# One decode of the expert picks for eight heads in 16 bits, in place of two for four heads in 32 bits

## The chip, the cores and the metric

One core of one Trainium2 chip runs the whole program as one launch. The metric is the device time of that launch in microseconds; the median of several runs counts. Times inside a profile are counted from the first instruction (the span's start).

## What is computed

Two decoder blocks over 256 tokens of width 1024. The first ends in a feed-forward layer of 16384 experts, of which every token uses 16 for each of 8 heads. The part that matters here, cut from the reference:

```python
def peer_ffn(xn, wq, subkeys, u_tab, v_tab):
    q = (xt @ wq).reshape(T, PEER_HEADS, 2, PEER_HALF)
    s = jnp.einsum('thpd,hpnd->thpn', q, subkeys).astype(jnp.float32)
    top_s, top_i = lax.top_k(s, PEER_TOPK)                     # 16 of 128 row keys, 16 of 128 column keys
    cand_s = (top_s[:, :, 0, :, None] + top_s[:, :, 1, None, :]).reshape(...)
    cand_i = (top_i[:, :, 0, :, None] * PEER_NKEYS + top_i[:, :, 1, None, :]).reshape(...)
    best_s, best_j = lax.top_k(cand_s, PEER_TOPK)              # 16 of the 256 pairs
    idx = jnp.take_along_axis(cand_i, best_j, axis=-1)
    gates = jax.nn.softmax(best_s, axis=-1)
    def retrieve(args):
        uc, vc = u_tab[ic], v_tab[ic]
        hdn = jax.nn.gelu(jnp.einsum('cd,chkd->chk', xc, uc), approximate=False) * gc
        return jnp.einsum('chk,chkd->cd', hdn, vc)
```

The kernel does not gather. It multiplies all experts with all tokens ("ups", table `peer_u`), weighs each hidden unit with a dense gate that is zero for experts not picked, and multiplies with the second table ("downs", `peer_v`).

## The kernel before, in words

Matrix products of 32-bit weights are made from a high and a low part: ScalarE writes `whi` from the loaded slice `raw`, VectorE or GpSimd the rest `wlo` = `raw` - `whi` (`split_next`, line 452). Each slice has 128x1024 numbers; four raw slices and four split pairs fit. Weights are loaded and split in the fixed order of the list `order`, ahead of their use.

The program is written out by one planner, `Flow` (line 107), which keeps a model clock per engine. Matrix work comes from a list of jobs. Beside them run chains (Python generators); after each piece of matrix work the planner steps every chain whose time has come by the model clock of TensorE. `yield 0` waits until the model says that the chain's last results are there, `yield SOON` lets it go on 1.2 us before that. So the order of instructions on each engine is fixed when the program is built; on the chip, engines wait for one another's data.

The feed-forward layer goes so. The query products of the 8 heads come first. For every head, `top_keys` (line 1597) scores the keys; `best16` (line 1579) finds the 16 best with VectorE's max and index instructions; GpSimd adds the 56 candidate pairs that can win into `cd`, and `best16` picks 16 of them into `bs` (values) and `bj` (positions, 0 to 63). After head 7 the two chains `decode(0)` and `decode(1)` (line 1629) follow one another, each for four heads. A decode

- subtracts the largest value (`g_`), and takes from the position, by shifts, casts, comparisons and small products on [128, 2, 16, 4] tiles, which of the 16 row keys and of the 16 column keys it names (`row`, `cl`): 25 VectorE instructions, lines 1637 to 1675;
- looks the key numbers up, in four passes (two token halves, row and column): compare `row` or `cl` with the constant table `io16` (filled by GpSimd in `top_keys` for head 1, line 1600), multiply with the 16 key numbers `il`, add the 16 products in halves, write into `GI` (lines 1678 to 1692). These run on 16-bit tiles of [128, 16, 64];
- makes Exp of `g_` on ScalarE, and on VectorE the softmax sum, the gate and its rest behind 16 bits (lines 1694 to 1703).

After the second decode TensorE transposes the eight parts of `GI`, and ScalarE writes them into `GT` (lines 1706 to 1713). `ex["gates"]` counts these steps; at 3 `swap_pools` (line 1899) gives the decode's memory to the gate tiles, and `dense_gates` (line 1877) starts. It builds the dense gates in four blocks of 32 key rows. `gate_steps` (line 1827) makes, for 8 tokens at a time, the one-hot tiles `oq`, `oe` and `op` on VectorE, and TensorE multiplies them: 16 small products for block 0, a "burst"; ScalarE copies them out into `gd`. A block has 32 such steps.

The order of the experts is given by hand (lines 893 to 897): ups 0 to 21 (`LEAD` 16 plus `AHEAD` 6), then downs 0 to 5, then up and down in turn. Down 0 waits until block 0 is built (`ex["built"]`, line 1804); `weigh` (line 1739) multiplies the hidden units with the gates on VectorE and makes the high part `ah` on ScalarE and the low part `al` on VectorE. Block 1 may start after six downs (line 1884) and is needed for down 16. From the first decode to the last gate block all `wlo` are VectorE's (`pool_free`, line 464).

Of the kernel before, what the change touches and what calls it, by code (L numbers as in the profile page):

```python
# [10 lines left out]
F32 = mybir.dt.float32  # L11
F32R = mybir.dt.float32r
F16 = mybir.dt.float16
# [299 lines left out]
def tile_blocks(ctx: ExitStack, tc: tile.TileContext, a, out):  # L313
# [32 lines left out]
    def bank(tag="sm"):  # L346
        return psum["tiles"].tile([128, 512], F32, name=tag, tag=tag, bufs=psum[tag])
# [13 lines left out]
    def cst(name):  # L361
        k, s, e = TABS[name]
        return tabs[k][:, s:e]
# [1175 lines left out]
    def open_c():  # L1539
        nonlocal sk, io16, v16, i16, bs, bj, GI  # L1540
        pa.__exit__(None, None, None)
        banks(4, 4)
        Bt.open(tc.tile_pool(name="pbt", bufs=1, side="right", reuse_waits="tile"))
        sk = Bt.tile([128, 16, 128], F32, name="sk")
        nc.scalar.dma_start(sk, a["sk"])
        io16 = Bt.tile([128, 16, 64], F16, name="io16")
        v16 = Bt.tile([128, 2, 16, 16], F32, name="v16")
        i16 = Bt.tile([128, 2, 16, 16], U32, name="i16")
        bs = Bt.tile([128, 2, 8, 16], F32, name="bs")
        bj = Bt.tile([128, 2, 8, 16], U32, name="bj")  # L1550
        GI = [Bt.tile([128, 4, 2, 64], F32, name="GI%d" % tt) for tt in range(2)]
        yield


# [42 lines left out]
    def top_keys(h, q):  # L1597
        yield lambda: ex["top"] == h and ex["best"] >= h - 1 and ex["sums16"] >= h - 2
        if h == 1:
            G.tensor_copy(io16, cst("iota16")[:, :, None].to_broadcast([128, 16, 64]))  # L1600
        b = bank()
        for tt in range(2):
            for p_ in range(2):
                o = (tt * 2 + p_) * 128
                mm(b[:, o:o + 128], q[:, p_, tt * 128:(tt + 1) * 128], sk[:, 2 * h + p_, :])
        s_ = Bt.tile([128, 4, 128], F32, name="s_", tag="s_", bufs=2)
        S.activation(s_, b4(b), AF.Copy)
        ex["top"] += 1
        yield 0
        yield lambda: ex["best"] == h  # L1610
        yield from best16([(v16[:, tt, 2 * h + p_, :], i16[:, tt, 2 * h + p_, :], s_[:, tt * 2 + p_, :])
                for tt in range(2) for p_ in range(2)], 128)
        ex["best"] += 1


        cd = Bt.tile([128, 2, 64], F32, name="cd", tag="cd", bufs=2)
        for i0, n, w, o in ((0, 1, 16, 0), (1, 3, 8, 16), (4, 4, 4, 40), (8, 8, 1, 56)):
            G.tensor_tensor(cd[:, :, o:o + n * w].rearrange("p t (i j) -> p t i j", i=n),
                            v16[:, :, 2 * h, i0:i0 + n, None].to_broadcast([128, 2, n, w]),
                            v16[:, :, 2 * h + 1, None, 0:w].to_broadcast([128, 2, n, w]), op=OP.add)  # L1620
        yield 0
        yield lambda: ex["sums16"] == h
        yield from best16([(bs[:, tt, h, :], bj[:, tt, h, :], cd[:, tt, :]) for tt in range(2)], 64)
        ex["sums16"] += 1
        if h == 7:
            for g in range(2):
                flow.spawn(decode(g))

    def decode(g):

        yield lambda: ex["gates"] == g
        ex["pool_free"] = False
        hs = slice(4 * g, 4 * g + 4)

        g_ = Bt.tile([128, 2, 16, 4], F32, name="g_", tag="g_")
        bt = bs[:, :, hs, :].rearrange("p t h k -> p t k h")
        V.tensor_tensor(g_, bt, bt[:, :, 0:1, :].to_broadcast([128, 2, 16, 4]), op=OP.subtract)

        def t(name, dt=F32):
            return Bt.tile([128, 2, 16, 4], dt, name=name, tag=name)  # L1640

        ip, i2, i3 = t("ip", U32), t("i2", U32), t("i3", U32)
        V.tensor_copy(ip, bj[:, :, hs, :].rearrange("p t h k -> p t k h"))
        V.tensor_scalar(i2, ip, 2, None, op0=OP.logical_shift_right)
        V.tensor_scalar(i3, ip, 3, None, op0=OP.logical_shift_right)
        yield SOON
        f1, f2, f3, fp = t("f1"), t("f2"), t("f3"), t("fp")
        V.tensor_copy(fp, ip)
        V.tensor_copy(f2, i2)
        V.tensor_copy(f3, i3)  # L1650

        V.tensor_scalar(f1, fp, 16.0, None, op0=OP.is_ge)
        m2, m3, d, c = t("m2"), t("m3"), t("d"), t("c")
        V.tensor_scalar(m2, fp, 40.0, None, op0=OP.is_ge)
        V.tensor_scalar(m3, fp, 56.0, None, op0=OP.is_ge)
        yield SOON
        row, cl = t("row", F16), t("cl", F16)
        V.tensor_tensor(d, f2, f3, op=OP.subtract)
        V.scalar_tensor_tensor(d, d, -5.0, m2, op0=OP.add, op1=OP.mult)
        V.scalar_tensor_tensor(c, f3, -1.0, f1, op0=OP.add, op1=OP.mult)  # L1660
        V.tensor_tensor(d, d, c, op=OP.add)
        yield SOON
        V.tensor_tensor(c, fp, f2, op=OP.subtract)
        V.scalar_tensor_tensor(c, c, -42.0, m3, op0=OP.add, op1=OP.mult)
        V.tensor_tensor(row, d, c, op=OP.add)
        V.tensor_tensor(f1, f1, f3, op=OP.mult)
        yield SOON
        V.scalar_tensor_tensor(d, f3, -2.0, f2, op0=OP.mult, op1=OP.add)
        V.tensor_tensor(d, d, m2, op=OP.mult)
        V.scalar_tensor_tensor(c, f2, -4.0, fp, op0=OP.mult, op1=OP.add)  # L1670
        V.tensor_tensor(c, c, m3, op=OP.mult)
        yield SOON
        V.scalar_tensor_tensor(f1, f1, -8.0, fp, op0=OP.mult, op1=OP.add)
        V.scalar_tensor_tensor(f1, d, -4.0, f1, op0=OP.mult, op1=OP.add)
        V.tensor_tensor(cl, f1, c, op=OP.subtract)
        yield 0
        S.activation(g_, g_, AF.Exp)
        for tt in range(2):
            for w in range(2):
                il = Bt.tile([128, 16, 4], F16, name="il", tag="il", bufs=2)  # L1680
                V.tensor_copy(il, i16[:, tt].rearrange("p (h w) c -> p w c h", w=2)[:, w, :, hs])
                at = (row, cl)[w][:, tt].rearrange("p k h -> p (k h)")
                eq = Bt.tile([128, 16, 64], F16, name="eq", tag="eq", bufs=2)
                V.tensor_tensor(eq, io16, at[:, None, :].to_broadcast([128, 16, 64]), op=OP.is_equal)
                e4 = eq.rearrange("p c (k h) -> p c k h", h=4)
                V.tensor_tensor(e4, e4, il[:, :, None, :].to_broadcast([128, 16, 16, 4]), op=OP.mult)
                yield SOON
                n = 8
                while n > 1:
                    V.tensor_tensor(eq[:, 0:n, :], eq[:, 0:n, :], eq[:, n:2 * n, :], op=OP.add)  # L1690
                    n //= 2
                V.tensor_tensor(GI[tt][:, 2 + w, g, :], eq[:, 0, :], eq[:, 1, :], op=OP.add)
                yield SOON
        gs = Bt.tile([128, 2, 4], F32, name="gs", tag="gs")
        V.tensor_reduce(gs, g_.rearrange("p t k h -> p t h k"), axis=AX.X, op=OP.add)
        V.reciprocal(gs, gs)
        V.tensor_scalar(gs, gs, 16384.0, None, op0=OP.mult)
        for tt in range(2):
            V.tensor_tensor(GI[tt][:, 0, g, :].rearrange("p (k h) -> p k h", h=4), g_[:, tt],
                            gs[:, tt, None, :].to_broadcast([128, 16, 4]), op=OP.mult)  # L1700
            hi16 = Bt.tile([128, 64], F16, name="hi16", tag="hi16")
            V.tensor_copy(hi16, GI[tt][:, 0, g, :])
            V.tensor_tensor(GI[tt][:, 1, g, :], GI[tt][:, 0, g, :], hi16, op=OP.subtract)
            yield SOON
        ex["gates"] += 1
        if g == 1:
            yield 0
            for tt in range(2):
                b = bank()
                for w in range(4):  # L1710
                    tr(b[:, w * 128:(w + 1) * 128], GI[tt][:, w].rearrange("p g k -> p (g k)"))
                S.activation(GT[:, :, tt * 128:(tt + 1) * 128, :], b4(b)[:, :, :, None].to_broadcast([128, 4, 128, 2]), AF.Copy)
            ex["gates"] += 1

    GH, AH = {}, {}

# [180 lines left out]
            yield from (up, down)[w](i)  # L1897

    def swap_pools():
        yield lambda: ex["gates"] == 3  # L1900
        Bt.close()
        ex["pbg"] = tc.tile_pool(name="pbg", bufs=1, side="right", reuse_waits="tile")
        ex["pool"] = ex["pbg"].__enter__()
        ex["ahead"] = ex["pool"].tile([128, NB // 2, 2, 256], F32, name="ahead", tag="gd", bufs=2)
# [451 lines left out]
```

## Time and profile before

| what | us |
|---|---|
| median of 3 runs (1687.53 to 1687.61) | 1687.54 |
| the profiled execution | 1684.77 |
| its span, first to last instruction | 1683.0 |
| TensorE busy in the span | 1628.0 (97%) |
| VectorE busy | 1238.0 (74%) |
| ScalarE busy | 738.1 (44%) |
| GpSimd busy | 206.4 (12%) |

PE is TensorE, DVE is VectorE, ACT is ScalarE, POOL is GpSimd, PEld is TensorE's loading of weights. All instructions that go through the planner carry the line of its helper (L264; L344 for matrix products, L369 for transposes), so rows are told apart by the names of their tiles: the output before `<-`, the inputs behind it. A duration covers an instruction to its last write; the next one on VectorE starts a little earlier. Matrix products overlap; their spacing is their cost.

### The profile page before, as it was taken

How to read it: one execution, taken by the hardware profiler on the slowest of the kernel's cores; microseconds unless marked ns; L12 is line 12 of the kernel's file. 1: busy time of each engine (PE TensorE's matmuls, PEld its weight loads, DVE VectorE, ACT ScalarE, POOL GpSimd, SP SyncE). 2: the span in 40 equal slices, each digit the busy share in tenths (PEclk: the TensorE clock that was granted, in tenths of full speed). 3: DMA queues.
4: the chain of work that ended last, by engine and by line, in shares of the span. 5: the costliest groups of instructions: out<-in, count | busy, mean ns of one | idle time of the engine just before them, and what ended most of it. 6: DMA issues, size and time to landing. Idle time of an engine off the chain costs nothing.

```text
span 1683.0 us, 27724 instructions
## 1 busy us (share of the span) xinstructions
PE 1628.0 (97%) x10778; PEld 1405.6 (84%) x10778; DVE 1238.0 (74%) x2689; ACT 738.1 (44%) x1118; POOL 206.4 (12%) x157
## 2 busy tenths in 40 slices
PE   6999999999999999999999999999999999999997
PEld 5748888679998798889899898988798777998885
DVE  6698865369989788988957888477558756656666
ACT  1332321145554455445544555454443444555452
POOL 0042211068000000000000000401123100000000
PEclk9999999999999899999999999999999999999999
DMA  9562334455654455545566665666764464553442
GB/s 382 171 209 92 103 111 151 157 168 154 192 168 129 127 175 175 175 147 177 159 207 190 187 189 187 201 201 187 240 187 146 142 202 143 170 151 120 124 150 88
DMA packets 78616, 283.31 MB, mean 168 GB/s; under 512 B 9106, under 2 KB 9362, under 8 KB 77844
## 3 DMA queue, kind: packets, MB, share of 16 engines
q1 hardware_dynamic: 77188, 276.81, 52.4%
q10 hardware_dynamic: 1296, 4.72, 0.8%
q8 instruction: 84, 1.38, 0.3%
q14 instruction: 48, 0.39, 0.1%
HBM read 280.45 MB, written 1.05 MB: 167 GB/s over the span
## 4 chain that ended last, share of the span: by engine, by line
PE 88%; DVE 8%; ACT 2%; issue 1%; DMA 1%; POOL 0%; ACTq 0%; DVEq 0%; SPq 0%; POOLq 0%
PE mm L344 53%; PE sm L344 33%; PE sm L369 1%; DVE wlo L264 1%; ACT whi L264 1%; DVE op L264 1%; DVE oq L264 0%; DVE h L264 0%; DVE x L264 0%; DVE ny L264 0%; DVE acc L264 0%; DVE n_r L264 0%; DMA xs<-in_x 0%; DVE ma L264 0%; DMA raw<-in_ada 0%
## 5 line engine op out<-in xcount | busy, mean ns | idle before, releaser
L264 DVE TENSOR_TENSOR wlo<-raw,whi 128x1024 fp32r<-128x1024 f32 (+1 forms) x381 | 469.3, 1237 | 172.0 <-ACT whi L264 170.4
L264 ACT ACTIVATE whi<-raw 128x1024 fp32r<-128x1024 f32 (+1 forms) x415 | 431.4, 1042 | 260.9 <-PE mm L344 129.9
L344 PE MATMUL sm<-xh,whi 128*128 128x256 f32 x1024 | 295.7, 289 | 0.0
L344 PE MATMUL sm<-xl,whi 128*128 128x256 f32 x1024 | 289.4, 283 | 0.0
L344 PE MATMUL sm<-xh,wlo 128*128 128x256 f32 x1024 | 289.2, 282 | 0.0
L344 PE MATMUL mm<-whi,ah 128*128 128x512 f32 x512 | 205.8, 402 | 5.2 <-ACT ah L264 5.2
L344 PE MATMUL mm<-wlo,ah 128*128 128x512 f32 x512 | 201.6, 394 | 0.0
L344 PEld LDWEIGHTS sm<-xl,whi 128*128 128x128 f32 x1024 | 196.0, 191 | 1.2
L344 PEld LDWEIGHTS sm<-xh,whi 128*128 128x128 f32 x1024 | 195.8, 191 | 1.2
L344 PEld LDWEIGHTS sm<-xh,wlo 128*128 128x128 f32 x1024 | 195.8, 191 | 0.0
L344 PE MATMUL mm<-whi,al 128*128 128x512 f32 x512 | 158.8, 392 | 0.0
L344 PEld LDWEIGHTS mm<-whi,ah 128*128 128x128 f32 x512 | 97.3, 190 | 23.5 <-ACT ah L264 5.5
L344 PEld LDWEIGHTS mm<-whi,al 128*128 128x128 f32 x512 | 96.9, 189 | 21.5
L344 PEld LDWEIGHTS mm<-wlo,ah 128*128 128x128 f32 x512 | 97.3, 190 | 18.3 <-DVE wlo L264 0.3
L264 POOL TENSOR_TENSOR gt<-gt,raw 128x640 f32<-128x640 f32 (+2 forms) x16 | 35.1, 2197 | 574.4 <-ACT raw L264 540.1
L264 POOL TENSOR_TENSOR wlo<-raw,whi 128x1024 fp32r<-128x1024 f32 x34 | 82.8, 2444 | 122.4 <-ACT whi L264 118.9
L344 PE MATMUL mm<-whi,xh 128*128 128x512 f32 (+1 forms) x240 | 96.5, 402 | 0.1
L344 PE MATMUL mm<-whi,xl 128*128 128x512 f32 (+1 forms) x240 | 93.3, 389 | 3.1 <-DVE xl L264 3.1
L344 PE MATMUL mm<-wlo,xh 128*128 128x512 f32 (+1 forms) x240 | 93.1, 388 | 2.6 <-POOL wlo L264 1.2
L344 PE MATMUL mm<-xh,whi 128*128 128x256 f32 x328 | 95.0, 290 | 0.0
L344 PE MATMUL mm<-xl,whi 128*128 128x256 f32 x328 | 92.8, 283 | 0.0
L344 PE MATMUL mm<-xh,wlo 128*128 128x256 f32 x328 | 92.8, 283 | 0.0
(544 smaller groups left out, 3053.6 us busy)
## 6 DMA issues: line engine op xcount, KB each, us to landing
raw<-in_peer_u SPq DMA_DIRECT2D x128, 512.0 KB, 3.8
raw<-in_peer_v SPq DMA_DIRECT2D x128, 512.0 KB, 4.5
raw<-in_ada SPq DMA_DIRECT2D x48, 512.0 KB, 5.0
raw<-in_wa_v SPq DMA_DIRECT2D x16, 512.0 KB, 4.9
raw<-in_wa_g SPq DMA_DIRECT2D x16, 512.0 KB, 4.0
raw<-in_wa_o SPq DMA_DIRECT2D x16, 512.0 KB, 4.2
raw<-in_wb_g SPq DMA_DIRECT2D x16, 512.0 KB, 3.9
raw<-in_wb_o SPq DMA_DIRECT2D x16, 512.0 KB, 4.3
```

The costliest lines, as they stand in the source:

```text
L264: return f(*args, **kw)
L344: P.matmul(o, l, r, start=first, stop=last)
L369: P.transpose(o, x, ident[0:x.shape[0], 0:x.shape[0]])
```

## The change

One `decode()` takes all eight heads. Its tiles have [128, 2, 16, 8] elements; the whole numbers that are not shifted (`f1` to `f3`, `fp`, `m2`, `m3`, `d`, `c`) are 16-bit floats. The lookup has four passes with tiles of [128, 16, 128] in place of eight with [128, 16, 64], so `io16` doubles. The softmax tail works on both token halves at once. Exp moves from behind the small steps to a place behind the shifts. The yields stand elsewhere: two are added inside each pass. `GI` is one tile. The count for `swap_pools` is 2 in place of 3.

```diff
-        io16 = Bt.tile([128, 16, 64], F16, name="io16")
+        io16 = Bt.tile([128, 16, 128], F16, name="io16")
...
-        GI = [Bt.tile([128, 4, 2, 64], F32, name="GI%d" % tt) for tt in range(2)]
+        GI = Bt.tile([128, 2, 4, 128], F32, name="GI")
...
-            G.tensor_copy(io16, cst("iota16")[:, :, None].to_broadcast([128, 16, 64]))
+            G.tensor_copy(io16, cst("iota16")[:, :, None].to_broadcast([128, 16, 128]))
...
-            for g in range(2):
-                flow.spawn(decode(g))
-
-    def decode(g):
-
-        yield lambda: ex["gates"] == g
+            flow.spawn(decode())
+
+    def decode():
+
         ex["pool_free"] = False
-        hs = slice(4 * g, 4 * g + 4)
...
-        def t(name, dt=F32):
-            return Bt.tile([128, 2, 16, 4], dt, name=name, tag=name)
+        def t(name, dt=F16):
+            return Bt.tile([128, 2, 16, 8], dt, name=name, tag=name)
+
+
+        g_ = t("g_", F32)
+        bt = bs.rearrange("p t h k -> p t k h")
+        V.tensor_tensor(g_, bt, bt[:, :, 0:1, :].to_broadcast([128, 2, 16, 8]), op=OP.subtract)
 
         ip, i2, i3 = t("ip", U32), t("i2", U32), t("i3", U32)
-        V.tensor_copy(ip, bj[:, :, hs, :].rearrange("p t h k -> p t k h"))
+        V.tensor_copy(ip, bj.rearrange("p t h k -> p t k h"))
         V.tensor_scalar(i2, ip, 2, None, op0=OP.logical_shift_right)
         V.tensor_scalar(i3, ip, 3, None, op0=OP.logical_shift_right)
         yield SOON
+        S.activation(g_, g_, AF.Exp)
...
-        yield 0
-        S.activation(g_, g_, AF.Exp)
         for tt in range(2):
             for w in range(2):
-                il = Bt.tile([128, 16, 4], F16, name="il", tag="il", bufs=2)
-                V.tensor_copy(il, i16[:, tt].rearrange("p (h w) c -> p w c h", w=2)[:, w, :, hs])
+                il = Bt.tile([128, 16, 8], F16, name="il", tag="il", bufs=2)
+                V.tensor_copy(il, i16[:, tt].rearrange("p (h w) c -> p w c h", w=2)[:, w])
                 at = (row, cl)[w][:, tt].rearrange("p k h -> p (k h)")
-                eq = Bt.tile([128, 16, 64], F16, name="eq", tag="eq", bufs=2)
-                V.tensor_tensor(eq, io16, at[:, None, :].to_broadcast([128, 16, 64]), op=OP.is_equal)
-                e4 = eq.rearrange("p c (k h) -> p c k h", h=4)
-                V.tensor_tensor(e4, e4, il[:, :, None, :].to_broadcast([128, 16, 16, 4]), op=OP.mult)
+                eq = Bt.tile([128, 16, 128], F16, name="eq", tag="eq", bufs=2)
+                yield SOON
+                V.tensor_tensor(eq, io16, at[:, None, :].to_broadcast([128, 16, 128]), op=OP.is_equal)
+                yield SOON
+                e4 = eq.rearrange("p c (k h) -> p c k h", h=8)
+                V.tensor_tensor(e4, e4, il[:, :, None, :].to_broadcast([128, 16, 16, 8]), op=OP.mult)
                 yield SOON
                 n = 8
                 while n > 1:
                     V.tensor_tensor(eq[:, 0:n, :], eq[:, 0:n, :], eq[:, n:2 * n, :], op=OP.add)
                     n //= 2
-                V.tensor_tensor(GI[tt][:, 2 + w, g, :], eq[:, 0, :], eq[:, 1, :], op=OP.add)
-                yield SOON
-        gs = Bt.tile([128, 2, 4], F32, name="gs", tag="gs")
+                V.tensor_tensor(GI[:, tt, 2 + w, :], eq[:, 0, :], eq[:, 1, :], op=OP.add)
+        yield SOON
+        gs = Bt.tile([128, 2, 8], F32, name="gs", tag="gs")
         V.tensor_reduce(gs, g_.rearrange("p t k h -> p t h k"), axis=AX.X, op=OP.add)
         V.reciprocal(gs, gs)
         V.tensor_scalar(gs, gs, 16384.0, None, op0=OP.mult)
+        V.tensor_tensor(GI[:, :, 0, :].rearrange("p t (k h) -> p t k h", h=8), g_, gs[:, :, None, :].to_broadcast([128, 2, 16, 8]), op=OP.mult)
+        hi16 = Bt.tile([128, 2, 128], F16, name="hi16", tag="hi16")
+        V.tensor_copy(hi16, GI[:, :, 0, :])
+        V.tensor_tensor(GI[:, :, 1, :], GI[:, :, 0, :], hi16, op=OP.subtract)
+        ex["gates"] += 1
+        yield 0
...
-        yield lambda: ex["gates"] == 3
+        yield lambda: ex["gates"] == 2
```

## Rows read from the trace of the kernel before

**Rows 1.** Windows: stretch and length, busy us by engine, PEclk, DMA share, GB/s

```profile
421.80:493.06 71.26, 71.26 (x594) 71.01 (x593) 65.36 (x150) 37.56 (x44) 3.03 (x2) 1.00 0.61 187
497.06:538.70 41.64, 41.64 (x598) 40.64 (x596) 40.84 (x102) 20.77 (x37) 0.00 (x0) 1.00 0.46 135
538.70:552.28 13.58, 7.21 (x163) 5.66 (x162) 13.27 (x39) 4.33 (x11) 0.00 (x0) 0.63 0.17 58
554.76:559.75 4.99, 4.99 (x12) 3.99 (x13) 3.46 (x4) 1.57 (x2) 1.62 (x2) 0.54 0.01 3
560.00:590.00 30.00, 30.00 (x135) 24.87 (x134) 21.23 (x22) 14.33 (x17) 1.85 (x3) 1.00 0.61 186
720.00:730.00 10.00, 8.20 (x44) 6.69 (x45) 8.12 (x16) 3.99 (x7) 0.00 (x0) 0.83 0.23 77
```

**Rows 2.** Timeline of TensorE: start, us, instruction, count, idle before and releaser

```profile
536.04 0.57 PE L344 MATMUL sm<-op,oq 128*128 128x32 f16 x16
536.46 0.36 PE L344 MATMUL sm<-xh,whi 128*128 128x256 f32 x1
...
538.70 1.03 PE L344 MATMUL sm<-op,oq 128*128 128x32 f16 x32
...
552.13 0.76 PE L344 MATMUL sm<-op,oq 128*128 128x32 f16 x16 [0.58 <-DVE op L264]
554.76 0.80 PE L344 MATMUL mm<-whi,ah 128*128 128x512 f32 x1 [1.86 <-ACT ah L264]
...
559.75 0.39 PE L344 MATMUL mm<-whi,ah 128*128 128x512 f32 x1
...
561.14 0.39 PE L344 MATMUL mm<-whi,ah 128*128 128x512 f32 x1
```

**Rows 3.** The chain that ended last, around the first down: start, us, what

```profile
552.93 0.39 ACT gd L264
553.35 0.70 DVE gh L264
554.08 0.64 ACT ah L264
554.76 35.10 PE mm L344 x144
```

**Rows 4.** Groups of VectorE by form, 421.8 to 493.2: busy us, mean ns, idle before

```profile
L264 DVE TENSOR_TENSOR wlo<-raw,whi 128x1024 fp32r<-128x1024 f32 x24 | 29.3, 1221 | 3.7 <-ACT whi L264 3.4 <-issue 0.2
L264 DVE TENSOR_TENSOR eq<-eq,il 128x1024 f16<-128x1024 f16 x8 | 5.5, 692 | 0.3
...
L264 DVE TENSOR_TENSOR eq<-eq 128x128 f16<-128x128 f16 x8 | 1.8, 226 | 0.3
...
L264 DVE SCALAR_TENSOR_TENSOR c<-f,f 128x128 f32<-128x128 f32 x2 | 0.6, 285 | 0.0
...
L264 DVE TENSOR_TENSOR d<-f,f 128x128 f32<-128x128 f32 x2 | 0.6, 284 | 0.0
```

**Rows 5.** VectorE's windows: the four stretches of small steps, second decode

```profile
458.50:459.53 1.03, 0.93 (x6) 1.00 0.76 155
...
sum 5.87, DVE 5.50; mean DVE 1.37
```

**Rows 6.** VectorE's windows: the four passes, two stretches each, second decode

```profile
469.48:470.93 1.45, 1.42 (x4) 1.00 0.37 82
...
sum 10.56, DVE 10.01; mean DVE 1.25
```

**Rows 7.** VectorE's windows: the two stretches of gate tail, second decode

```profile
sum 2.13, DVE 1.89; mean DVE 0.94
```

**Rows 8.** Timelines of GpSimd and VectorE near head 1

```profile
363.80 1.04 POOL L264 CAST io<-cona 128x1024 f16<-128x1024 f32 x1
...
368.58 0.87 DVE L264 MAX8 v<-s__2763 128x8 f32<-128x128 f32 x4 [7.73 <-ACT s__2763 L264]
```

**Rows 9.** Waits of TensorE from 560 to 1100: us, times, longest

```profile
PE mm L344 <- ACT ah L264: 3.4, 1, 3.4
```

More of the change, by code (lines that the diff above doesn't have):

```diff
@@ L1625, in top_keys @@
         if h == 7:
-            for g in range(2):
-                flow.spawn(decode(g))
-    def decode(g):
-        yield lambda: ex["gates"] == g
+            flow.spawn(decode())
+    def decode():
         ex["pool_free"] = False
-        hs = slice(4 * g, 4 * g + 4)
-        g_ = Bt.tile([128, 2, 16, 4], F32, name="g_", tag="g_")
-        bt = bs[:, :, hs, :].rearrange("p t h k -> p t k h")
-        V.tensor_tensor(g_, bt, bt[:, :, 0:1, :].to_broadcast([128, 2, 16, 4]), op=OP.subtract)
-        def t(name, dt=F32):
-            return Bt.tile([128, 2, 16, 4], dt, name=name, tag=name)
+        def t(name, dt=F16):
[3 more added lines that the diff above has]
+        V.tensor_tensor(g_, bt, bt[:, :, 0:1, :].to_broadcast([128, 2, 16, 8]), op=OP.subtract)
         ip, i2, i3 = t("ip", U32), t("i2", U32), t("i3", U32)
-        V.tensor_copy(ip, bj[:, :, hs, :].rearrange("p t h k -> p t k h"))
+        V.tensor_copy(ip, bj.rearrange("p t h k -> p t k h"))
         V.tensor_scalar(i2, ip, 2, None, op0=OP.logical_shift_right)
@@ L1656, in decode @@
         yield SOON
-        row, cl = t("row", F16), t("cl", F16)
+        row, cl = t("row"), t("cl")
         V.tensor_tensor(d, f2, f3, op=OP.subtract)
@@ L1661, in decode @@
         V.tensor_tensor(d, d, c, op=OP.add)
+        V.tensor_tensor(c, fp, f2, op=OP.subtract)
         yield SOON
-        V.tensor_tensor(c, fp, f2, op=OP.subtract)
         V.scalar_tensor_tensor(c, c, -42.0, m3, op0=OP.add, op1=OP.mult)
@@ L1666, in decode @@
         V.tensor_tensor(f1, f1, f3, op=OP.mult)
-        yield SOON
         V.scalar_tensor_tensor(d, f3, -2.0, f2, op0=OP.mult, op1=OP.add)
         V.tensor_tensor(d, d, m2, op=OP.mult)
+        yield SOON
         V.scalar_tensor_tensor(c, f2, -4.0, fp, op0=OP.mult, op1=OP.add)
         V.tensor_tensor(c, c, m3, op=OP.mult)
-        yield SOON
         V.scalar_tensor_tensor(f1, f1, -8.0, fp, op0=OP.mult, op1=OP.add)
@@ L1691, in decode @@
                     n //= 2
-                V.tensor_tensor(GI[tt][:, 2 + w, g, :], eq[:, 0, :], eq[:, 1, :], op=OP.add)
-                yield SOON
-        gs = Bt.tile([128, 2, 4], F32, name="gs", tag="gs")
+                V.tensor_tensor(GI[:, tt, 2 + w, :], eq[:, 0, :], eq[:, 1, :], op=OP.add)
+        yield SOON
+        gs = Bt.tile([128, 2, 8], F32, name="gs", tag="gs")
         V.tensor_reduce(gs, g_.rearrange("p t k h -> p t h k"), axis=AX.X, op=OP.add)
@@ L1697, in decode @@
         V.tensor_scalar(gs, gs, 16384.0, None, op0=OP.mult)
-        for tt in range(2):
[L1699 to L1704, printed above, removed]
-        ex["gates"] += 1
[L1706 to L1713, printed above, removed]
+        V.tensor_tensor(GI[:, :, 0, :].rearrange("p t (k h) -> p t k h", h=8), g_, gs[:, :, None, :].to_broadcast([128, 2, 16, 8]), op=OP.mult)
[4 more added lines that the diff above has]
+        yield 0
+        for tt in range(2):
+            b = bank()
+            for w in range(4):
+                tr(b[:, w * 128:(w + 1) * 128], GI[:, tt, w])
+            S.activation(GT[:, :, tt * 128:(tt + 1) * 128, :], b4(b)[:, :, :, None].to_broadcast([128, 4, 128, 2]), AF.Copy)
+        ex["gates"] += 1
     GH, AH = {}, {}
```

## The prediction

> **What bounds the kernel now.** I read the windows first, then the timeline of TensorE, then the chain, then the rows of VectorE. TensorE bounds the program: in the 71.26 us in which the picks are decoded (421.80 to 493.06) it is busy from end to end, and again in the 41.64 us of gate building behind them [rows 1]. So nothing that VectorE does in those two stretches is paid for there. The bill comes right behind: from 538.70 to 552.28 TensorE is busy 7.21 us of 13.58, VectorE 13.27, and the granted clock is 0.63 of full speed [rows 1]. The timeline shows why. The expert "up" products end at 538.70; what follows is two gate bursts, then nine rows of one burst each with a wait on VectorE's `op` tile (0.58 us before the last), and at 554.76 the first "down" product, which waited for `ah` [rows 2]. The wait is the planned one: a down may start when gate block 0 is complete, the block may start when the decode has ended, and the 22 ups that the order sets ahead of the first down are used up. VectorE is the server of this queue: it is 92% busy in the decode (65.36 of 71.26), 98% in the gates [rows 1].
>
> The pause costs more than its length. After it the clock is 0.54 until 559.75 [rows 1]: two groups of six down products take 554.76 to 559.75, 4.99 us, where the next group takes 559.75 to 561.14, 1.39 us [rows 2]. That is 4.99 - 2 x 1.39 = 2.2 us lost to the lower of the clock's two levels (1.2 GHz for 2.4).
>
> **What could be gained at most.** The eleven bursts behind 538.70 have to be done anyway. At full clock one takes 536.04 to 536.46, 0.42 us [rows 2], so they need 4.6 us: TensorE is through with ups and bursts at 543.3. Behind that stand the eviction of the last up and the making of `ah`: nothing if both are hidden, 1.4 us for the steps in the chain (gates times hidden units at 553.35, `ah` at 554.08, product at 554.76 [rows 3]). So the first down could start at 543.3 to 544.7 instead of 554.76.
>
> **The change on VectorE, by steps.** Two prices per element come from rows of one pattern at two sizes. 16-bit tensors: 692 ns at 1024 and 226 at 128, 0.52 ns an element. 32-bit tensors: 1221 at 1024 and 284 at 128, 1.05 ns [rows 4]. An instruction taken twice as wide costs its added elements and saves the other one whole.
>
> - Small steps, 25 a decode: 5.87 us for four heads [rows 5], 11.74 for both. At eight heads each has 128 elements more. The 32-bit subtraction adds 0.13 us. Six shifts, copies and casts from whole numbers add 0.07 to 0.13 each, taken as 0.6. Three comparisons add 0 to 0.07 each, taken as 0.1. Eight two-tensor steps, now 16-bit, add nothing (256 x 0.52 = 128 x 1.05). For the seven steps with two operations and two tensors no row shows a 16-bit form: between 0 (packed like the two-tensor rows) and 0.13 each (one element at a time). I take 0.13, since no row shows them packed: 0.9 us. New sum 7.6 us, saving 4.1. The ends: 6.4 if all are packed, 9.0 if none is.
> - Compare, multiply and sum, eight passes: four cost 10.56 us [rows 6], 2.64 each, 21.1 in all. Four passes stay, each with 2,944 more 16-bit elements (1.53 us), and 64 more in the cast and in the last sum (0.12): 4.29 each, 17.2 in all. Saving 3.9.
> - Gate tail: 2.13 us a decode [rows 7], 4.26 for both. One at eight heads: 192 more elements in the three steps per token half that become one (0.55), 128 more in the sum (0.13), less the steps dropped: 2.2. Saving 2.1.
>
> Together VectorE does 10.1 us less (8.7 to 11.3 with the ends above).
>
> **The rest of the diff.** One pair of ScalarE table loads and one Exp go; ScalarE is busy 37.56 of 71.26 us there [rows 1], so I count nothing. If Exp, moved ahead, stands before its input is ready, the splits `whi` behind it on ScalarE are late, and VectorE's `wlo` with them; in the decode TensorE has the weights of several slices ahead, which covers some us. The constant table `io16` doubles on GpSimd: 1.04 us at 363.80 becomes 2.1, while VectorE has nothing to do until 368.58 [rows 8]: nothing. The eight transposes and the two evictions into `GT` stay. No DMA is issued or moved. The decode's wait between the two groups goes; the 24 splits (`wlo`) that VectorE makes between its steps [rows 4] stay, and the added yields let them in between the wider steps.
>
> **The sum.** VectorE's gate work now ends at 552.28 and was idle for only 1.1 us in the last 55 us (40.84 + 13.27 busy of 41.64 + 13.58 [rows 1]), so 10.1 us less ends it at 542.2. Its last burst (0.42), its eviction (553.35 - 552.93 = 0.42) and the chain (554.76 - 553.35 = 1.41 [rows 3]) put the first down at 544.5. TensorE is free at 543.3, with the eviction of the last up and `ah` behind it at about 544.7. Both roads meet there: 554.76 - 544.7 = 10.1 us, and with so short a pause the 2.2 us of low clock go too. From there to the end TensorE paces, so 12.3 us arrive at the end. The profiled execution (1684.77, span 1683.0) lies 2.8 us under the median of the runs; the difference is taken off the median: 1687.54 - 12.3 = **1675.2 us**. With the ends: 1.4 us more if eviction and `ah` are hidden, 1673.8; 1.5 us less by the saving of 8.7, and 2.2 less if the clock falls all the same, 1679.
>
> A rule weighed: the rows show the two-operation form at 285 ns beside 284 for the two-tensor form, both 128 elements of 32 bits [rows 4], so it runs at the same rate. The Trainium skill, Vector Engine (DVE) Microarchitecture Reference, section "Points that are easy to get wrong", says that this form with two SBUF sources that aren't bf16 runs at half throughput. That speaks against the change, since f16 isn't bf16; the 285 ns disagree with it. By it the seven steps would cost an estimated 1.9 us more, and the sum would be 1677.
>
> **Rivals.**
> - B, the freed time is passed on in part. VectorE idles 5.90 of the 71.26 us of the decode [rows 1], in waits for splits that TensorE paces; lighter decode steps may only lengthen those. If half of the 10.1 us arrives, the first down starts 5 us earlier and the clock falls for half as long: 6 us, 1681.5. Against it: the gates behind the decode keep VectorE busy, and take up what it has.
> - C, more than that. A second pause, 3.4 us for `ah` [rows 9], stands before gate block 1, with clock 0.83 over the 10 us around it (1.7 us) [rows 1]. If the new order happens to remove it: 1675.2 - 5.1 = 1670.1. Against it: block 1 starts six downs after the first down, and both move together.
> - D, no change within 0.2%. The pause now lets loads run ahead (58 GB/s in it [rows 1]). Were the loads the next to be late, the pause would return as a wait for weights: 1687.5. Against it: from 560 to 590 TensorE is busy throughout while 186 GB/s arrive [rows 1].
> - E, slower: the wider steps lose the packed rate. In the four passes 5,888 elements each would cost 0.52 ns more, 12.2 us, and the eight two-tensor steps and comparisons 1.3 us; the 10.1 us saved turn into 3.4 lost, straight onto the pause: 1691. It decides from 10.1 us of extra cost on. Against it: the 16-bit rows hold 0.52 ns at 1024 elements, with the same broadcasts [rows 4].
>
> **How the numbers follow.** A 0.62 (1675.2), B 0.17, C 0.07, D 0.08, E 0.06. Two runs of this kernel can tell a difference over about 0.2%, 3.4 us. A, B and C are faster by more: 0.86; D is the same: 0.08; E slower: 0.06. The range takes in C at the low end and B at the high end: 1670 to 1682, leaving out D, E and the worst of B.
>
> **What would show it.** Right: the nine rows of lone gate bursts are gone or stand among ups; the first `mm<-whi,ah` follows the last up by under 2 us beyond its bursts and lies near 544.7; the clock stays at 1.00 through 560; the decode has 65 VectorE instructions fewer (59 for 124) and ends near 473: 36.1 us of its 65.36 are not splits (24 x 1.22), 26 remain, and at the same share of the time 71.26 us become 51. That is more than 10.1 us because only the time between splits is its own. The compare and multiply at 128x2048 take 1.2 us each; the seven two-operation steps 0.3 to 0.4. Wrong: 2.3 us for a compare (E), lone bursts that are still there with VectorE idle in the decode (B), waits for `raw` in 545 to 600 (D).

## The result, and the profile after

The changed kernel takes 1673.28 us (median of 6 runs, 1672.53 to 1674.11), the kernel before 1686.55 beside it (6 runs, 1683.29 to 1687.61): a ratio of 0.9926, with a 95% interval of 0.9916 to 0.9936. By the ratio that is a gain of 12.5 us (the two medians lie 13.3 apart); 12.3 were forecast. The profiled executions are 1673.86 (span 1672.1) and 1684.77 (span 1683.0), 10.9 us apart.

The profile page of the changed kernel, its line of engines (busy us, share of the span, instructions):

```profile
PE 1624.1 (97%) x10778; PEld 1403.1 (84%) x10778; DVE 1228.3 (73%) x2624; ACT 734.7 (44%) x1115; POOL 207.2 (12%) x157
```

VectorE went from 2689 instructions to 2624, the 65 that the prediction counted, and from 1238.0 us busy to 1228.3. TensorE's busy time fell too, from 1628.0 to 1624.1, with the same 10778 products: the first sign that some of them now run at the higher clock.

Windows of the changed kernel, columns as in [rows 1]. The first is the decode, the second the gates up to the start of the last burst, the third from there to the first down, the fourth the first downs (as long as the low-clock window of before), the last two belong to what comes later:

```profile
422.61:470.25 47.64, 47.64 (x399) 47.64 (x399) 45.87 (x76) 23.71 (x27) 3.00 (x2) 1.00 0.60 188
475.37:537.30 61.93, 61.87 (x884) 60.29 (x882) 60.03 (x145) 31.00 (x55) 0.00 (x0) 1.00 0.44 142
537.30:546.06 8.76, 7.56 (x76) 7.31 (x75) 4.03 (x5) 4.10 (x6) 0.00 (x0) 1.00 0.53 160
546.05:551.04 4.99, 4.99 (x22) 4.14 (x23) 4.04 (x5) 2.64 (x3) 1.62 (x2) 1.00 0.22 84
560.00:590.00 30.00, 30.00 (x170) 25.82 (x169) 22.91 (x36) 15.13 (x18) 0.61 (x1) 1.00 0.56 179
710.00:720.00 10.00, 9.08 (x52) 7.47 (x52) 7.90 (x16) 5.10 (x7) 0.00 (x0) 0.83 0.21 61
```

Against [rows 1], the decode takes 47.64 us instead of 71.26 for the two of before, the clock is 1.00 where it was 0.63 and 0.54, and VectorE, 98% busy ahead of the first down before, is busy 4.03 us of the last 8.76. Loads bring 160 and 179 GB/s behind the gates, and among TensorE's waits from 560 to 1100 (3.3 us for `ah`, 0.5 for `op`) none is for a load.

TensorE's timeline of the changed kernel, at the places of [rows 2] (the last burst, the last up, the first downs):

```profile
537.36 0.57 PE L344 MATMUL sm<-op,oq 128*128 128x32 f16 x16
...
544.57 0.28 PE L344 MATMUL sm<-xh,wlo 128*128 128x256 f32 x1
546.05 0.50 PE L344 MATMUL mm<-whi,ah 128*128 128x512 f32 x1 [1.20 <-ACT ah L264]
...
548.90 0.39 PE L344 MATMUL mm<-whi,ah 128*128 128x512 f32 x1
```

The last burst now stands among the ups, 7 us ahead of the last up's end. The nine rows of lone bursts are gone, and what is left of the pause is 1.20 us for `ah`. The first two groups of six downs take 546.05 to 548.90, 2.85 us, where they took 4.99. The chain that ended last, in the changed kernel, shows what now sets the first down:

```profile
529.92 14.94 PE sm L344 x172
544.86 0.02 issue
544.88 0.60 ACT ahead L264
545.48 0.53 ACT ah L264
546.01 0.04 issue
546.05 14.12 PE mm L344 x61
```

In [rows 3] `gh` on VectorE stood in this place; now it is TensorE's own last up, its eviction (`ahead`) and `ah`. The rest of VectorE's side is this, its timeline in the changed kernel from the last gate steps on:

```profile
535.75 0.49 DVE L264 TENSOR_TENSOR op<-oe,GT 128x256 f16<-128x256 f16 x2
537.03 1.23 DVE L264 TENSOR_TENSOR wlo<-raw,whi 128x1024 fp32r<-128x1024 f32 x1 [0.78 <-ACT whi L264]
540.70 1.22 DVE L264 TENSOR_TENSOR wlo<-raw,whi 128x1024 fp32r<-128x1024 f32 x1 [2.45 <-ACT whi L264]
542.98 1.23 DVE L264 TENSOR_TENSOR wlo<-raw,whi 128x1024 fp32r<-128x1024 f32 x1 [1.05 <-ACT whi L264]
544.12 0.68 DVE L264 TENSOR_TENSOR gh<-gh,gd 128x512 f32<-128x512 f32 x1
```

The last gate step ends at 536.24, and VectorE then idles 0.78 + 2.45 + 1.05 = 4.3 us ahead of `gh`. That slack is a number to test: it says how much of the saved time was more than could be used.

Where the saved time came from, in VectorE's groups by form in the decode (422.6 to 470.3) of the changed kernel, columns as in [rows 4]:

```profile
L264 DVE TENSOR_TENSOR wlo<-raw,whi 128x1024 fp32r<-128x1024 f32 x16 | 19.5, 1220 | 0.8 <-ACT whi L264 0.7
L264 DVE TENSOR_TENSOR eq<-eq,il 128x2048 f16<-128x2048 f16 x4 | 4.9, 1220 | 0.0
L264 DVE TENSOR_TENSOR eq<-io,cl 128x2048 f16<-128x2048 f16 x2 | 2.4, 1219 | 0.0
L264 DVE CAST f<-i 128x256 f16<-128x256 uint32 x2 | 0.5, 286 | 0.0
L264 DVE SCALAR_TENSOR_TENSOR c<-f,f 128x256 f16<-128x256 f16 x1 | 0.4, 419 | 0.0
L264 DVE TENSOR_TENSOR d<-f,f 128x256 f16<-128x256 f16 x1 | 0.3, 279 | 0.0
```

Compare and multiply at 2048 elements take 1.22 us, where [rows 4] have 692 ns at 1024: still 0.52 ns for each added element. A two-tensor step in 16 bits costs 279 ns for 256 elements, where 128 in 32 bits cost 284. The two-operation step costs 419. And VectorE waited 0.7 us for `whi` here, where [rows 4] have 3.4. The wait at the handover from the decode to the gates, which [rows 4] leave out, is still there in the changed kernel:

```profile
473.98 1.22 DVE L264 TENSOR_TENSOR wlo<-raw,whi 128x1024 fp32r<-128x1024 f32 x1 [2.60 <-ACT whi L264]
```

One pair of rows sums up VectorE's splits from the start of the decode to the end of its gate work, in the kernel before (421.80 to 552.40) and in the changed one (422.60 to 536.30):

```profile
L264 DVE TENSOR_TENSOR wlo<-raw,whi 128x1024 fp32r<-128x1024 f32 x36 | 43.9, 1220 | 6.3 <-ACT whi L264 6.0 <-issue 0.2
L264 DVE TENSOR_TENSOR wlo<-raw,whi 128x1024 fp32r<-128x1024 f32 x33 | 40.1, 1219 | 3.4 <-ACT whi L264 3.3
```

Three splits fewer stand in this stretch, and 2.9 us less of waiting ahead of them.

The windows that answer to the sums of [rows 5, 6, 7], in the changed kernel: small steps in five stretches, one pass, the tail:

```profile
sum 6.78, DVE 6.47; mean DVE 1.29
sum 4.29, DVE 4.15; mean DVE 1.38
sum 2.31, DVE 2.14; mean DVE 2.14
```

The subtraction at the decode's start is left out of the first, since it runs beside two `wlo` on GpSimd and takes 3.48 us (3.25 for half the size before); without that company it took 0.39 before, so an estimated 0.42 here, and the small steps come to 7.2. With four passes at 4.29 and 2.3 for the tail the decode's own work is 26.7 us against 11.74 + 21.1 + 4.26 = 37.1.

### The profile page after: what moved, and what is told of

Its sections match the earlier page's. It is cut to its first block, busy times and chain, and to the rows that moved or that the text cites. A ratio compares the mean times of both kernels' runs of the same rounds, so it can differ in the third digit from the quotient of the medians.

```text
span 1672.1 us, 27655 instructions
## 1 busy us (share of the span) xinstructions
PE 1624.1 (97%) x10778; PEld 1403.1 (84%) x10778; DVE 1228.3 (73%) x2624; ACT 734.7 (44%) x1115; POOL 207.2 (12%) x157
## 3 DMA queue, kind: packets, MB, share of 16 engines
HBM read 280.45 MB, written 1.05 MB: 168 GB/s over the span
## 4 chain that ended last, share of the span: by engine, by line
PE 88%; DVE 8%; ACT 2%; issue 1%; DMA 1%; POOL 0%; ACTq 0%; DVEq 0%; SPq 0%; POOLq 0%
PE mm L344 53%; PE sm L344 33%; PE sm L369 1%; DVE wlo L264 1%; ACT whi L264 1%; DVE oq L264 1%; DVE op L264 0%; DVE h L264 0%; DVE x L264 0%; DVE ny L264 0%; DVE acc L264 0%; DVE n_r L264 0%; DMA xs<-in_x 0%; DVE ma L264 0%; DMA raw<-in_ada 0%
## 5 line engine op out<-in xcount | busy, mean ns | idle before, releaser
L264 DVE TENSOR_TENSOR al<-gh,ah 128x512 fp32r<-128x512 f32 x64 | 48.7, 761 | 60.3 <-ACT ah L264 60.3
```

The costliest lines, as they stand in the source:

```text
L264: return f(*args, **kw)
```

## The experiments

Each kernel has 4 to 11 timed runs. They come in three sets, and in these the kernel before had medians of 1684.39, 1685.07 and 1684.99 us. A ratio is always to the kernel before in the same set. "First down" below is the time from the subtraction that begins the decode to the first `mm<-whi,ah`: 132.94 us before, 123.44 in the changed kernel. The decode's start itself lies between 420.8 and 423.4 in these runs, behind work that the edits leave as it was but for the filling of `io16`.

**Which part of the change does it: 16 bits or one decode?** First 16 bits alone, in the kernel before.

```diff
-        def t(name, dt=F32):
+        def t(name, dt=F16):
```

> The kernel before with its whole numbers in 16 bits, still two decodes of four heads. Theory A (VectorE's finish of gate block 0 sets the first down, and the change works by halving the number of instructions): at 128 elements only the fixed part is left to save, about 0.07 us on each of 16 two-tensor steps, 1.1 us in all; time 1 us under the kernel before, that is ratio 0.9993, no more than 0.998. Rival (the 16 bits carry the gain): ratio near 0.993 as for the whole change.

Measured: 1680.42 us, ratio 0.9971 (0.996 to 0.9982), first down 127.94. The steps became lighter by the amount expected, but the first down came 5.0 us earlier, not about 1.2, and the time is under the 0.998 that was held for the least. The form groups of this kernel's decodes give the prices at 128 elements:

```profile
L264 DVE SCALAR_TENSOR_TENSOR c<-f,f 128x128 f16<-128x128 f16 x2 | 0.6, 284 | 0.0
...
L264 DVE TENSOR_TENSOR d<-f,f 128x128 f16<-128x128 f16 x2 | 0.4, 218 | 0.0
```

The two-operation form gains nothing from 16 bits. The rest came from idle time. VectorE's waits ahead of splits in the two decodes fell from 3.64 us (3.4 for `whi`, 0.23 without a releaser) to 2.2, and at the handover to the gates this row of the kernel before's VectorE timeline

```profile
495.91 1.23 DVE L264 TENSOR_TENSOR wlo<-raw,whi 128x1024 fp32r<-128x1024 f32 x1 [2.63 <-ACT whi L264]
```

became this, in the kernel with 16 bits alone:

```profile
489.55 1.23 DVE L264 TENSOR_TENSOR wlo<-raw,whi 128x1024 fp32r<-128x1024 f32 x1
490.69 0.22 DVE L264 CAST irow<-cona 128x128 f16<-128x128 f32 x1
491.02 0.69 DVE L264 TENSOR_TENSOR oq<-irow,GT 128x1024 f16<-128x1024 f16 x1
```

In the kernel before, ScalarE's half of this split stood behind the two evictions into `GT`:

```profile
493.00 1.93 ACT L264 ACTIVATE GT<-sm 128x1024 f16<-128x1024 f32 x2
494.81 1.07 ACT L264 ACTIVATE whi<-raw 128x1024 fp32r<-128x1024 f32 x1
```

With 16 bits it stands ahead of them, at 488.46, and the gates follow without a wait. 1.2 of work, 1.4 and 2.6 of waits make 5.2, against 5.0 in the first down.

Then one decode alone, with its numbers in 32 bits:

```diff
-        def t(name, dt=F16):
+        def t(name, dt=F32):
...
-        row, cl = t("row"), t("cl")
+        row, cl = t("row", F16), t("cl", F16)
```

> The changed kernel with its whole numbers in 32 bits, one decode of eight heads. Theory A: eight two-tensor steps and three comparisons cost 0.13 and 0.07 us more, 1.3 us; VectorE has 4.3 us of idle time between the last gate step and the first down after the change, which covers it: ratio to the kernel before 0.9926, as for the whole change. Rival (the 16 bits carry the gain): ratio 0.997 or more.

Measured: 1674.67 us, 0.9941 (0.9928 to 0.9955), first down 123.57, with the same 1.2 us for `ah`. One decode alone reaches the same first down; in it the 16 bits are more than can be used. The time lies a little above the ratio that was expected (0.9926) and far under the rival's 0.997.

**How much of the saving is used?** VectorE's time in the decode is raised again, by unread products of 1.22 us, four and then twelve (the diff shows four).

```diff
+        for _ in range(4):
+            yield SOON
+            V.tensor_tensor(Bt.tile([128, 16, 128], F16, name="eq", tag="eq", bufs=2), io16, io16, op=OP.mult)
```

> The changed kernel with four products of 128x2048 that nobody reads behind the lookup, 4.6 us of VectorE. Theory A: the 4.3 us of idle time take it; at most 1 us slower than the changed kernel, ratio to the kernel before 0.9926 to 0.9935. Rival (VectorE still sets the first down after the change): 4.6 us slower, ratio 0.9953.

> The changed kernel with twelve such products, 13.7 us of VectorE. Theory A: 13.7 less 4.3 us of idle time, 9.4 us of pause, and 2.2 us of low clock come back: 11.6 us slower than the changed kernel, ratio to the kernel before 0.9995, with lone gate bursts before the first down and the clock at 0.5 to 0.6 behind them. Rival (the pause before had another cause, and the gain came from elsewhere): ratio stays under 0.996.

With four, 4.9 us more: 1675.34 us, 0.9942 (0.9928 to 0.9956), first down 123.78, only 0.3 later. The timed ratio is higher than expected, and its interval holds both the upper end of the expectation and the rival's 0.9953; it is the first down in the trace that decides. With twelve, 14.6 us more: 1686.12, 1.0009 (1.0 to 1.0019), first down 133.47, 10.0 later. The slack of 4.3 us read above takes the first 4.3; 14.6 - 4.3 = 10.3 arrive, against 10.0 measured. The time excludes the rival (under 0.996) and lies somewhat above the 0.9995 that was expected. TensorE's waits from 530 to 560 with twelve, and the windows of the same kernel around the pause:

```profile
PE sm L344 <- DVE op L264: 6.9, 10, 1.7
PE mm L344 <- ACT ah L264: 1.9, 1, 1.9
```

```profile
540.00:550.00 10.00, 5.67 (x127) 4.32 (x125) 9.72 (x31) 2.87 (x8) 0.00 (x0) 0.59 0.13 45
550.00:560.00 10.00, 7.22 (x48) 5.70 (x49) 5.96 (x11) 3.66 (x7) 1.62 (x2) 0.56 0.04 6
```

The pause of before is back, with its waits on `op`, its VectorE at 97% and its low clock. The other direction: the column lookup is left out (two of four passes; a copy stands in for them, so the kernel picks other experts).

```diff
-            for w in range(2):
+            for w in range(1):
...
+            V.tensor_copy(GI[:, tt, 3, :], cl[:, tt].rearrange("p k h -> p (k h)"))
```

> The changed kernel without the lookup of the column keys: two of four passes are left out, and the column numbers of the decode stand in for the key numbers. VectorE does 8 us less. Theory A (TensorE's own work sets the first down now, the gain is used up): ratio to the kernel before 0.992, within 1 us of the changed kernel. Rival (VectorE still sets it): 8 us faster than the changed kernel, ratio 0.988.

Measured: 1673.97 us, 0.9926 (0.9912 to 0.9939), first down 122.96. Some 8 us less work is worth 0.5 us: what VectorE's decode had to give in this place has been given.

**What is the clock worth?** In the kernel before, unread products keep TensorE busy through the pause. The first form puts them into the bank of the gate products, whose values it changes.

```diff
+                if ex.get("ups") == LEAD + AHEAD:
+                    for _ in range(6):
+                        mm(b[:, 256:512], xn2[0][:, 0, 0:128], xn2[0][:, 0, :])
```

> The kernel before with six products of 128x256 that nobody reads behind each gate burst once the last up is out (0.7 us of TensorE per burst, in place of its idle time). The first down comes when it came. Theory A with its second term (2.2 us of the 12.3 are the low clock behind the pause): the clock stays at 1.0, ratio 0.9987 (2.2 us). Rival (the low clock costs nothing, or the pause hides it): ratio 1.000 or more.

Measured: 1685.38 us, 0.9998 (0.9989 to 1.0007). The clock is 1.00 from 540 to 560 and the first two groups take 2.83 us instead of 4.99, but the fillers behind the last burst put the first down 0.7 later. So a second form has a bank of its own and none behind the last burst:

```diff
+                ex["bursts"] = ex.get("bursts", 0) + 1
+                if ex.get("ups") == LEAD + AHEAD and ex["bursts"] < 32:
+                    if "fill" not in ex:
+                        ex["fill"] = bank("mm")
+                    for _ in range(6):
+                        mm(ex["fill"][:, 0:256], xn2[0][:, 0, 0:128], xn2[0][:, 0, :])
```

> The kernel before with six products of 128x256 that nobody reads behind each gate burst from the last up on, in a bank of their own and not behind the last burst. The first down comes when it came. Theory A: clock 1.0 behind the pause, 2.2 us faster, ratio 0.9987. Rival: ratio 1.000 or more.

Measured: 1683.72 us, 0.9995 (0.9986 to 1.0004), first down 132.87, as before. Its windows of the pause and of the first downs:

```profile
539.82:553.40 13.58, 12.63 (x217) 11.60 (x216) 13.24 (x39) 4.31 (x11) 0.00 (x0) 1.00 0.17 58
555.81:560.80 4.99, 4.99 (x22) 4.14 (x23) 4.04 (x5) 2.64 (x3) 1.62 (x2) 1.00 0.00 0
```

With TensorE kept busy the clock stays at the higher level, and two groups take 555.81 to 558.67, 2.86 us: 2.1 less than in [rows 2]. The profile thus shows the 2.2 us that the prediction charged to the clock. The timed runs don't resolve it: the interval holds both 0.9987 (2.2 us) and no change.

**What made the waits go?** The prediction left VectorE's idle time as it was, and within the decode it fell, from 3.64 us ahead of splits to 0.72. One possible cause is the place of Exp on ScalarE, which the change moves ahead; here it alone moves, in the kernel before:

```diff
         yield SOON
+        S.activation(g_, g_, AF.Exp)
...
-        yield 0
-        S.activation(g_, g_, AF.Exp)
```

> The kernel before with Exp of each decode behind the shifts, where the change puts it, and nothing else. Theory A with waits: in the kernel before VectorE idles 1.0 us in each decode for a split that ScalarE makes late, behind Exp and its two table loads; if the new place avoids both, 2 us of VectorE's time go, straight off the pause: ratio 0.9988. Rival (these waits depend on where the splits fall, not on Exp): ratio 1.000 within 1 us.

Measured: 1685.31 us, 1.0 (0.9991 to 1.0009), first down 132.91. The waits ahead of splits are 3.4 us in the decodes (3.64 before) and 2.64 at the handover (2.63 before). Exp's place is worth nothing that these runs can tell. The other runs narrow it down. With 16 bits alone 2.2 us of waits are left in the decodes, with one decode in 32 bits 0.66, so the one decode is enough for it. The wait at the handover is another matter: 2.76 us with one decode in 32 bits, 2.60 in the changed kernel, and gone only with 16 bits alone, where the split stood ahead of the evictions. The one decode also brings two added yields in each pass, which give the splits other places. Wider steps and yields were not tried apart, so which of them shortened the waits is not shown.

**Is the place of the first down itself the next thing to choose?** `AHEAD` is the number of ups that the order puts ahead of the first down beside `LEAD` (22 - 16 = 6). With VectorE's gate work over at 536.24 and TensorE's last up at 544.86, one of these ups can be handed back; before the change, more of them could cover the pause.

```diff
-AHEAD = 6
+AHEAD = 5
```

> The changed kernel with five ups ahead in place of six. Theory A: the gates are built about 8 us before the last up ends, so the up given away (5.8 us) costs no pause; gate block 1 may start one down earlier against down 16, has 11.2 us more, and the second pause (3.3 us and some 1.7 us of low clock) goes: 4 to 5 us faster than the changed kernel, ratio to the kernel before 0.990. Rival (the second pause has another cause, or the first comes back): ratio 0.9926 or more.

> The changed kernel with four ups ahead in place of six. Theory A: the second pause stays away as with five, but a second up (5.8 us) is given away, where the gates are finished only 3 to 4 us before they are needed with five: the first pause comes back by 2 to 4 us, and perhaps the low clock; slower than with five ups (0.989) by 2 to 5 us, ratio to the kernel before 0.990 to 0.992. Rival (fewer ups ahead is simply better): ratio 0.988 or less.

> The kernel before with eight ups ahead in place of six. Theory A: the two more ups (11.5 us) fill the first pause without any change to the decode, with at most 2 us of pause left and the clock at 1.0; but gate block 1 may start only two downs later against down 16 and has 22 us less, so the second pause grows, by 10 us or more: ratio 1.000 to 1.008. Rival (the first pause isn't a lack of TensorE work): lone bursts before the first down stay.

The changed kernel with 5: **1668.11 us**, 0.989 (0.9874 to 0.9905), the best of all. First down 117.65, 5.8 earlier (the up given back), still with 1.2 us for `ah`. From 620 to 1100 one wait of TensorE is left. The stretch of the second pause in the windows (columns as in [rows 1]) is this in the changed kernel with 6

```profile
705.00:720.00 15.00, 11.65 (x74) 9.84 (x72) 12.26 (x26) 6.38 (x9) 0.00 (x0) 0.89 0.35 110
```

and this with 5:

```profile
705.00:720.00 15.00, 15.00 (x127) 13.54 (x126) 13.73 (x28) 7.50 (x11) 0.00 (x0) 1.00 0.51 161
```

The second pause [rows 9] is gone: 3.3 us of waiting and, by an estimate from 0.83 over 10 us, 1.7 of clock make 5.0. The medians of the two kernels lie 5.2 us apart, or 5.7 by the repeated run below. With 4 the second pause stays away, but the first is back: 1674.36 us, 0.9935 (0.9921 to 0.9949), slower than the 0.990 to 0.992 expected, and TensorE's waits from 520 to 560 are

```profile
PE sm L344 <- DVE op L264: 2.1, 2, 1.5
PE mm L344 <- ACT ah L264: 1.9, 1, 1.9
```

with a clock of 0.62 over the 7.7 us behind them. The kernel before with 8: 1682.84 us, 0.9983 (0.9974 to 0.9992), a little faster, where no gain was expected, since the second pause was expected to grow by 10 us or more. Two more ups nearly fill the first pause (3.1 us of waits remain; the added ups bring splits of their own onto VectorE) but the second one grows, by some 4 us. TensorE's waits from 600 to 1100 in it:

```profile
PE sm L344 <- DVE op L264: 5.7, 6, 1.3
PE mm L344 <- ACT ah L264: 2.3, 1, 2.3
```

TensorE's waits in this later part are thus 8.0 us with 8 (in the kernel before), 3.8 with 6 and 0.5 with 5. Gate block 1 may begin only when `AHEAD` downs have been done (the condition at the head of each block in `dense_gates`), which would explain it; this cause was not tried apart from the order of the ups that `AHEAD` also sets.

Last, the changed kernel again, unaltered, beside the others of the third set:

> The changed kernel again, on the chip of these runs: ratio 0.9926, as a measure of how far ratios of different calls may be compared.

1673.85 us, 0.9932 (0.9918 to 0.9945): first down 123.42, waits of 1.2 and 3.4 us. The ratios of this one kernel in two sets differ by 0.0006.

## Why the prediction was right, and where it was not

- **The bound, and the place of the bill: right.** VectorE's finish of gate block 0 set the first down. Three kernels show it from both sides: 14.6 us of VectorE's work added bring the old first down back (133.47 for 132.94), 4.9 added or 8 taken away move it by 0.3 and 0.5 us. Two more ups in the kernel before show it from TensorE's side: the waits of the first pause fall to 3.1 us.
- **VectorE's sum: right.** Small steps 7.2 us (7.6 said), a pass 4.29 (4.29), tail 2.3 (2.2): 10.4 us less, for 10.1.
- **The two-operation form: the end taken was right.** 419 ns at 256 elements against 284 at 128 is 0.135 us each, 1.05 ns for every added element as in 32 bits. The two-tensor step in 16 bits adds half of that (218 to 279 ns). In 32 bits the two forms cost the same, 285 and 284 ns [rows 4]. The Trainium skill, Vector Engine (DVE) Microarchitecture Reference, section "Points that are easy to get wrong", halves the rate of this form for two SBUF sources that aren't bf16. The 32-bit rows disagree with it; in 16 bits the form runs at half the rate of the two-tensor step, but no slower than in 32 bits, so the 1.9 us that the rule would have added did not come.
- **"10.1 us less ends it at 542.2": the step that failed.** VectorE's gate work ended at 536.2, or, counted from the decode's start, 16.8 us earlier (552.28 - 421.80 = 130.5 to 113.6). The step carried VectorE's idle time and the splits ahead of its end over unchanged. Neither stood still. The waits ahead of splits fell by 2.9 us, all of it in the decode (3.64 to 0.72), and 33 splits stand in the stretch where 36 stood: those of the last slices, the three `wlo` at 537.03 to 544.21, are now behind the gate work. At their spacing of 1.14 us (542.98 to 544.12) they are 3.4 us of it. With the 10.4 us of work that makes 16.7 of the 16.8. That the moment at which a split is asked for decides how long it is waited for is read from the rows (16 bits alone: 2.6 us at the handover for little work); why the waits in the decode fell stays open, as said above. Rival B expected longer waits, and they became shorter. It also counted all of VectorE's 5.90 idle us as waits for splits, where [rows 4] have 3.7.
- **Why the forecast held all the same.** It said that two roads meet at the first down, and only the road over TensorE turned out to be the longer. That one was sized well: 1.20 us of pause for 1.4, and a first down 9.5 us earlier from the decode's start for 10.1. TensorE was through with ups and bursts 0.6 us later than eleven bursts at 0.42 made it. That the error on VectorE's road did no harm is luck: the prediction had the two roads meet within 0.2 us, and VectorE's was the shorter by 4.3 us, the slack read in the rows and borne out by the added products. Had it been the longer one, an error of that size would have been in the result. (The range's "1.5 us less by the saving of 8.7" is 1.1 by the prediction's own two roads; nothing hangs on it.)
- **The clock's 2.2 us: right in the rows.** The first two groups of downs went from 4.99 to 2.85 us, and with the filled pause in the kernel before to 2.86: 2.1 us, in rows only. From first down to the end of the span the time went from 1128.24 to 1126.05 us, 2.2 less, but it was 1127.35 in the repeated run, so this difference alone proves little. That a pause as short as 1.4 us leaves the clock up was assumed without a row; the changed kernel shows it for 1.20.
- **The decode's end: near.** 47.6 us after its start, for 51; the 2.9 us of waits are most of the difference.
- **The sum, against the runs.** 9.5 and 2.2 are 11.7. The decode started 0.8 later in the profile of after, which leaves 10.9, as the spans say. The timed gains, 12.5 us and 11.5 in the repeated run, lie on both sides of 11.7; the start of the decode alone varies by 2.6 us between profiles.
- **C, D and E** did not come. The second pause stayed (3.3 us, clock 0.83), since block 1 and the first down moved together, as argued; no product waited for `raw`; the 16-bit rate held at 2048 elements. C's price of 5.1 us was about right: one up fewer ahead collects 5.2 to 5.7.

## What to carry to other kernels

When an engine off the bound ends a planned wait too late, its time is paid one for one until the bounding engine's own road is the longer; read that second road first, since it caps the gain (here at 9.5 us, with 4.3 left as slack; one decode in 32 bits would have done). After such a change, look at the constants that the old lateness had set: here one fewer up ahead was worth another 5 us. One wider decode reached the whole gain without the smaller type: halving the instruction count saves the fixed part of every step (an estimated 0.15 us: 284 ns at 128 elements [rows 4] less 128 x 1.05). The smaller type alone brought 5.0 us of the first down, of which only 1.2 were lighter steps and the rest waits that happened to fall; under the wider decode nothing of it could be used. It helps only the forms that rows show to be faster in it.

## What the runs showed of the hardware that was not expected

- The same operation in 16 bits gains by its form: the two-tensor step went from 284 to 218 ns at 128 elements, the two-operation step stayed at 284, and at 256 they cost 279 and 419 ns.
- 1.2 us less work on VectorE brought the first down 5.0 us forward; 2.6 of them were a wait for a split that had stood behind two evictions in ScalarE's queue.
- A 32-bit subtraction of 0.39 us took 3.25 us (128 elements), and one of twice the size 3.48, beside two `wlo` on GpSimd: most of that time is not the operation's own.
- The granted clock stayed at 1.00 behind a pause of 1.2 us. It read 0.83 over the 10 us with a wait of 3.3, and 0.62 behind two waits of 2.1 us together and one of 1.9.
